# 3,680 unused bytes per partition below the MLP's tiles, in a two-layer diffusion backbone on one core

## The chip, the cores and the metric

One core of one Trainium2 chip. The metric is the device time of one execution in microseconds (us), median of the runs; lower is better. TensorE (PE) multiplies matrices, VectorE (DVE), ScalarE (ACT) and GpSimd (POOL) work elementwise, SyncE (SP) issues DMAs. PE reads two operands from the on-chip memory SBUF: the stationary one (the weights, loaded by LDWEIGHTS, shown as engine PEld) and the moving one, whose columns stream through. SBUF has 128 partitions; a tile's *address* below is its byte offset within each partition.

## The reference

Two layers run over 256 latent tokens and 256 context tokens of width 1024. Each layer ends in a squared-ReLU MLP, for both token streams in the first layer (512 tokens) and for the latent tokens alone in the last (256):

```python
def sqrelu_mlp(h, w1, w2):
    return jnp.square(jax.nn.relu(h @ w1)) @ w2
...
        x = x + mod[2][..., None, :] * (y @ w_out[l])
        x = x + mod[5][..., None, :] * sqrelu_mlp(ada_norm(x, g_mlp[l], mod[3], mod[4]), w_ff1[l], w_ff2[l])
```

`w_ff1` is 1024 x 4096 and `w_ff2` 4096 x 1024. Before the MLP stand a combined input projection (`w_in`), differential attention, latent attention, a bidirectional HGRN2 scan and an output projection (`w_out`).

## The kernel before

Activations are held with features on partitions and tokens along the free dimension, so a linear layer has the weights as stationary operand (128 x 128) and 512 or 256 tokens as moving operand. Every float32 product is made from three float32r products: weights and activations are each split into a high part and the rest, and `mm3` issues (weights x activations) high x high (L140), high x rest (L141) and rest x high (L142):

```python
139    def mm3(ps, lh, ll, rh, rl, start, stop):
140        PE.matmul(ps, lh, rh, start=start, stop=False)
141        PE.matmul(ps, lh, rl, start=False, stop=False)
142        PE.matmul(ps, ll, rh, start=False, stop=stop)
```

`wunit` (L120) fetches 512 KB of weights by a DMA on SP's queue into one of four `raw` buffers; ACT copies it to `wh` (L135, the high part), DVE subtracts to get `wl` (L136, the rest). `wh` and `wl` have three buffers each. `lin_fm` (L144) walks over such units: in the MLP a unit has 4 k-tiles of 256 output columns, so 24 matmuls (4 k-tiles x 2 column blocks x 3) read it.

The linear layers differ in the tile that they stream: the input projection reads `hh` and `hl`, the output projection `yh` and `yl`, the MLP's first product `mhh` and `mhl` (8 x 512 floats each; class `Norm` writes them), its second `fa` and `fb` (16 buffers each, written in `ev_ff`: L1334 and L1335). The MLP runs in two groups of 2048 hidden columns (L1318), each 16 units of `w_ff1` and then 16 of `w_ff2`: 64 units, 1,536 matmuls in a layer. In layer 0 `mod_beside` (L411) runs beside it on DVE: it sums the next layer's conditioning from `w_mod` (L424, L426), one DMA and two DVE instructions per step. The order on every engine is the order in which this Python issues.

The moving operand is 512 columns wide in layer 0 (`Tq` = 512). In layer 1 `fa` and `fb` are 256 wide; `mhh` and `mhl` are read through `Norm.gained`, which begins two columns early (L309, `x0 = self.T0 - 2`) to carry the shift vectors along: 258 columns from column 254 on.

Tiles come from stacked pools. The pool `wp` (raw, `wh`, `wl`, and `hh`, `hl`, `yh`, `yl`) is allocated once, low in SBUF. The pools of a layer's attention are closed before the MLP's pool opens (L1308), which then takes their place, directly above what stays. The built program places:

| tiles | address | modulo 4096 |
|---|---|---|
| `wh`, `wl` (three each, 4096 apart) | 88,960 to 109,440 | 2944 |
| `hh`, `hl`, `yh`, `yl` (16,384 each, k-tiles 2048 apart) | 56,192 and 72,576 | 2944, 896 |
| `mhh`, `mhl` (16,384 each, k-tiles 2048 apart) | 126,240 and 142,624 | 3360, 1312 |
| `fa`, `fb` of layer 0 (2048 each) | 159,008 to 222,496 | 3360, 1312 |
| `fa`, `fb` of layer 1 (1024 each) | 159,008 to 190,752 | 3360, 288, 1312, 2336 |
| the latent attention's `cqh`, `cql` and their weights `uqh` in layer 0 | 126,752 to 167,200, and 153,888 | |

A block of weights that a matmul loads begins 512 bytes after another inside `wh`, so all eight multiples of 512 occur as distances between weights and moving operand. The remainder by 512 does not change within a pool: `wh` lies at 384 modulo 512 and so do `hh`, `hl`, `yh`, `yl`; `mhh`, `mhl`, `fa` and `fb` at 288. In the latent attention `cqh`, `cql` and `uqh` all lie at 32 modulo 64, above the MLP pool's lower end.

Of the kernel before, what the change touches and what calls it, by code (L numbers as in the profile page):

```python
# [8 lines left out]
F32 = mybir.dt.float32  # L9
# [31 lines left out]
def net(ctx: ExitStack, tc, x, c, cx, c_ctx, w_mod, b_mod, g_mix, g_mlp, w_in, w_out, da_lambda, da_subln_g,  # L41
# [410 lines left out]
    def drain(g):  # L452
        for _ in g:
            pass
# [137 lines left out]
    def layer(l):  # L592
# [17 lines left out]
        def step(g):  # L610
            try:
                next(g)
                return True
            except StopIteration:
                return False
# [391 lines left out]
        def ev_res(gofs, k0, sq):  # L1007
            def ev(i, ps):
                k = k0 + i
                for r, a, b in streams:  # L1010
                    V.scalar_tensor_tensor(out=xT[:, k, a:b], in0=ps[:, a - T0q:b - T0q],
                                           scalar=modT[l][:, r, gofs + k:gofs + k + 1], in1=xT[:, k, a:b],
                                           op0=ALU.mult, op1=ALU.add)
                if sq:
                    sq_update(k, T0q)
            return ev
# [289 lines left out]


        with tc.tile_pool(name=f"mlp{l}", bufs=1) as fp:  # L1308
            NM = Norm(l, 1, T0q, fp.tile([128, KT, 512], F32R, name="mhh"), fp.tile([128, KT, 512], F32R, name="mhl"))
            drain(final)  # L1310
            beside = None if last else mod_beside(1)

            def run(g):
                for _ in g:
                    if beside:
                        next(beside, None)

            for grp in range(2):  # L1318
                hid = {}

                def ev_ff(j0):
                    def ev(i, ps, sp=None):
                        a = fp.tile([128, Tq], F32R, tag="fa", name="fa", bufs=16)
                        b = fp.tile([128, Tq], F32R, tag="fb", name="fb", bufs=16)
                        if sp is None:
                            t = ap_.tile([128, 512], F32, tag="ntmp", name="fr", bufs=2)
                            S.activation(out=t[:, 0:Tq], in_=ps, func=AF.Relu)
                        else:
                            t, c = NM.apply(ps, sp)
                            for r, x0, x1 in streams:  # L1330
                                tt = t[:, x0 - T0q:x1 - T0q]
                                S.activation(out=tt, in_=tt, func=AF.Relu, bias=c[:, r:r + 1])
                        V.tensor_mul(out=t[:, 0:Tq], in0=t[:, 0:Tq], in1=t[:, 0:Tq])
                        S.copy(out=a[:, 0:Tq], in_=t[:, 0:Tq])  # L1334
                        V.tensor_sub(out=b[:, 0:Tq], in0=t[:, 0:Tq], in1=a[:, 0:Tq].bitcast(F32))  # L1335
                        hid[j0 + i] = (a, b)
                    return ev

                if grp == 0:
                    drain(NM.first(w_ff1[l], [(0, 512)], ev_ff(0), not last))  # L1340
                for cc in range(0 if grp else 2, 8):
                    ev = ev_ff(2 * cc)
                    if last:
                        run(lin_fm(w_ff1[l], 0, [(2048 * grp + 256 * cc, 256)], KT, NM.gained, Tq + 2,
                                   lambda i, ps: ev(i, ps, 0)))
                    else:
                        run(lin_fm(w_ff1[l], 0, [(2048 * grp + 256 * cc, 256)], KT, NM.parts, Tq, ev))
                rhs_f = lambda k: (hid[k][0][:, 0:Tq], hid[k][1][:, 0:Tq])
                for cc in range(4):
                    g = lin_fm(w_ff2[l], 2048 * grp, [(256 * cc, 256)], 16, rhs_f, Tq, ev_res(40, 2 * cc, grp == 1))  # L1350
                    if last and grp and cc == 3:
                        step(g)
                        step(g)
                        obs = [fp.tile([128, 1024], F32, name=f"ob{t}") for t in range(2)]
                        final_rows(range(6), obs)
                    run(g)
            if beside:
                drain(beside)
            if last:
                final_norm(obs)  # L1360
# [4 lines left out]
    def final_rows(ks, obs):  # L1365

        for k in ks:
            S.activation(out=xT[:, k, 256:], in_=xT[:, k, 256:], func=AF.Copy, scale=vT2[:, k:k + 1])
        for t in range(2):
            for k in ks:  # L1370
                h = t, k // 4
                if h not in turned_x:
                    turned_x[h] = psum("mm" if k // 4 else "sc")
                PE.transpose(turned_x[h][:, 128 * (k % 4):128 * (k % 4) + 128], xT[:, k, 256 + 128 * t:384 + 128 * t], ident)
        if ks[0] == 0:
            for t in range(2):
                (V.tensor_copy, S.copy)[t](out=obs[t][:, 0:512], in_=turned_x[t, 0])

    def final_norm(obs):
        ss = stats([acc_state["a"], acc_state["b"]], 2)  # L1380
        r = rstd_small(ss, 2, DM)
        final_rows(range(6, 8), obs)
        for t, q in enumerate((nc.sync, nc.scalar)):
            V.tensor_scalar(out=obs[t][:, 0:512], in0=obs[t][:, 0:512], scalar1=r[:, t:t + 1], scalar2=None, op0=ALU.mult)
            S.activation(out=obs[t][:, 512:1024], in_=turned_x[t, 1], func=AF.Copy, scale=r[:, t:t + 1])
            for hf in range(2):
                q.dma_start(out=out[0, 128 * t:128 * t + 128, 512 * hf:512 * hf + 512], in_=obs[t][:, 512 * hf:512 * hf + 512])

    fillers += [mod_group(0, 1), mod_group(0, 2)]
    layer(0)  # L1390
    fill_all()
    layer(1)


# [49 lines left out]
```

## Time and profile before

| | us |
|---|---|
| median of 3 runs | 1242.29 (1239.74 to 1244.79) |
| the profiled execution, whole | 1242.65 |
| its span, from the first to the last instruction | 1240.9 |
| PE busy in the span | 1201.3 (97%) |
| layer 0's MLP, from its first matmul to its last | 404.46 to 782.02 |
| layer 1's MLP, likewise | 1046.44 to 1230.84 |

Times in the trace count from the span's start. A row of the timeline gives start and duration; matmuls overlap in a pipeline and their ends are modelled, so the pace of a stream is read from starts: last start minus first start, divided by the number of steps. This is called the **step** below.

### The profile page before, as it was taken

What the parts mean: (1) busy time and instruction counts of PE and PEld (TensorE: products, weight loads), DVE (VectorE), ACT (ScalarE), POOL (GpSimd) and SP (SyncE); (2) the same over time, 40 slices, a digit from 0 to 9 for tenths busy, and PEclk for the clock granted to TensorE, in tenths of its full rate; (3) what the DMA queues carried; (4) which work ended last, traced back from release to release, by engine and by line L of the source; (5) the groups of instructions that cost most, each with busy time, mean ns of one, the idle gap of its engine ahead of it and who ended that gap; (6) DMA issues with size and microseconds to landing.
All of it is one profiled execution on the core that took longest, in us unless ns stands there. A gap on an engine that the chain in (4) does not pass through costs nothing.

```text
span 1240.9 us, 21471 instructions
## 1 busy us (share of the span) xinstructions
PE 1201.3 (97%) x8318; PEld 963.9 (78%) x8318; DVE 888.5 (72%) x1786; ACT 584.4 (47%) x1114; POOL 111.4 (9%) x156
## 2 busy tenths in 40 slices
PE   6999999999999999999999999999998998999997
PEld 4677888755568777878787877788986668999997
DVE  4675587767776997765778673796788877865864
ACT  3534344576653654211233322464347874653653
POOL 2200000221200100000000000140003421000000
PEclk9999999999999999999999999999999998999999
DMA  9631213456543346555555554233324413555662
GB/s 324 187 86 49 76 53 105 119 158 198 189 153 107 98 139 198 188 154 159 178 155 162 164 169 134 68 103 99 94 58 121 126 32 119 175 184 187 187 187 69
DMA packets 138199, 170.93 MB, mean 138 GB/s; under 512 B 10883, under 2 KB 116033, under 8 KB 138097
## 3 DMA queue, kind: packets, MB, share of 16 engines
q1 hardware_dynamic: 134816, 164.08, 43.8%
q0 software_dynamic: 2704, 4.94, 1.6%
q8 instruction: 66, 1.08, 0.4%
q10 hardware_dynamic: 576, 0.53, 0.1%
q14 instruction: 37, 0.30, 0.1%
HBM read 160.21 MB, written 1.05 MB: 130 GB/s over the span
## 4 chain that ended last, share of the span: by engine, by line
PE 85%; DVE 7%; DMA 3%; ACT 3%; POOL 1%; issue 1%; ACTq 0%; POOLq 0%; SPq 0%
PE mm L142 21%; PE mm L140 21%; PE mm L141 21%; PE sc L1239 3%; PE sc L1225 2%; PE mm L392 2%; PE tp L907 2%; PE mm L219 2%; PE mm L218 2%; PE mm L220 2%; DMA mraw<-in_w_mod_dram 2%; PE sc L797 1%; DMA raw<-in_w_in_dram 1%; PE mm L930 1%; DVE wl L136 1%; PE sc L691 1%
## 5 line engine op out<-in xcount | busy, mean ns | idle before, releaser
L135 ACT CAST wh<-raw 128x1024 fp32r<-128x1024 f32 (+2 forms) x204 | 211.0, 1035 | 315.4 <-PE mm L141 244.9
L136 DVE TENSOR_TENSOR wl<-raw,wh 128x1024 fp32r<-128x1024 f32 (+2 forms) x201 | 242.9, 1209 | 127.5 <-ACT wh L135 124.7
L140 PE MATMUL mm<-mhh,wh 128*128 128x512 f32 (+1 forms) x512 | 174.0, 340 | 0.8 <-DVE fz L336 0.8
L140 PE MATMUL mm<-fa,wh 128*128 128x512 f32 (+1 forms) x512 | 173.7, 340 | 0.0
L142 PE MATMUL mm<-mhh,wl 128*128 128x512 f32 (+1 forms) x512 | 173.0, 339 | 0.4 <-DVE wl L136 0.4
L141 PE MATMUL mm<-mhl,wh 128*128 128x512 f32 (+1 forms) x512 | 173.3, 338 | 0.0
L141 PE MATMUL mm<-fb,wh 128*128 128x512 f32 (+1 forms) x512 | 173.3, 339 | 0.0
L142 PE MATMUL mm<-fa,wl 128*128 128x512 f32 (+1 forms) x512 | 173.2, 339 | 0.0
L426 DVE SCALAR_TENSOR_TENSOR room<-raw,scm,room 128x1024 f32<-128x1024 f32 x84 | 106.4, 1287 | 39.8 <-DMA raw<-in_w_mod_dram 39.8
L140 PE MATMUL mm<-hh,wh 128*128 128x512 f32 (+1 forms) x336 | 126.7, 382 | 4.6 <-ACT hh L351 3.3
L141 PE MATMUL mm<-hl,wh 128*128 128x512 f32 (+1 forms) x336 | 126.8, 378 | 2.3 <-DVE hl L352 2.3
L142 PE MATMUL mm<-hh,wl 128*128 128x512 f32 (+1 forms) x336 | 126.8, 378 | 1.1 <-DVE wl L136 1.1
L140 PEld LDWEIGHTS mm<-mhh,wh 128*128 128x128 f32 x512 | 96.2, 188 | 15.5 <-ACT wh L135 2.5
L140 PEld LDWEIGHTS mm<-fa,wh 128*128 128x128 f32 x512 | 96.3, 188 | 14.2 <-ACT wh L135 2.5
L142 PEld LDWEIGHTS mm<-mhh,wl 128*128 128x128 f32 x512 | 96.3, 188 | 12.5 <-DVE wl L136 0.8
L142 PEld LDWEIGHTS mm<-fa,wl 128*128 128x128 f32 x512 | 96.4, 188 | 11.7
L141 PEld LDWEIGHTS mm<-fb,wh 128*128 128x128 f32 x512 | 96.5, 189 | 11.6
L141 PEld LDWEIGHTS mm<-mhl,wh 128*128 128x128 f32 x512 | 96.3, 188 | 11.2
L140 PEld LDWEIGHTS mm<-hh,wh 128*128 128x128 f32 x336 | 63.5, 190 | 15.6 <-ACT hh L351 4.2
L141 PEld LDWEIGHTS mm<-hl,wh 128*128 128x128 f32 x336 | 64.2, 191 | 14.0 <-DVE hl L352 4.1
L142 PEld LDWEIGHTS mm<-hh,wl 128*128 128x128 f32 x336 | 64.0, 191 | 13.2 <-DVE wl L136 2.0
L347 POOL TENSOR_TENSOR nt<-nt,bc 128x256 f32<-128x256 f32 x24 | 27.0, 1132 | 493.5 <-ACT bc L326 445.5
(333 smaller groups left out, 2189.8 us busy)
## 6 DMA issues: line engine op xcount, KB each, us to landing
raw<-in_w_ff_dram SPq DMA_DIRECT2D x128, 512.0 KB, 3.8
raw<-in_w_mod_dram SPq DMA_DIRECT2D x80, 512.0 KB, 3.7
raw<-in_w_in_dram SPq DMA_DIRECT2D x42, 512.0 KB, 3.8
mraw<-in_w_mod_dram SPq DMA_DIRECT2D x32, 256.0 KB, 6.0
raw<-in_w_out_dram SPq DMA_DIRECT2D x10, 512.0 KB, 3.7
raw<-in_w_in_dram SPq DMA_DIRECT2D x16, 256.0 KB, 5.1
raw<-in_w_in_dram SPq DMA_DIRECT2D x8, 384.0 KB, 3.3
K<-dah POOLq DMA_DIRECT2D x48, 64.0 KB, 2.3
```

What stands on the lines that cost most here:

```text
L135: S.copy(out=wh, in_=raw)
L136: (low.pop() if low else V).tensor_sub(out=wl, in0=raw, in1=wh.bitcast(F32))
L140: PE.matmul(ps, lh, rh, start=start, stop=False)
L141: PE.matmul(ps, lh, rl, start=False, stop=False)
L142: PE.matmul(ps, ll, rh, start=False, stop=stop)
L218: PE.matmul(ps, a, wh[:, k, 0:w], start=st, stop=False)
L219: PE.matmul(ps, a, wl[:, k, 0:w], start=False, stop=False)
L220: PE.matmul(ps, b, wh[:, k, 0:w], start=False, stop=sp)
L347: G.tensor_mul(out=ts, in0=ts, in1=self.bc[:, a - T0:b - T0])
L392: PE.matmul(ps[32 * j:32 * j + 32, :], scm[:, k, :], raw[:, 512 * q:512 * q + 512], start=(k == 0), stop=(k == KT - 1))
L426: V.scalar_tensor_tensor(out=acc[r], in0=raw, scalar=scm[:, k, r:r + 1], in1=acc[r], op0=ALU.mult, op1=ALU.add)
L1239: PE.matmul(op[64 * r:64 * r + 64, 0:128], v[:, j, 64 * c:64 * c + 64], PT[:, js], start=(j == 0), stop=(j == nk - 1), tile_position=(0, 6 ...
```

## The change

Inside the MLP's pool, ahead of all its tiles, 920 floats per partition are allocated and never used:

```diff
         with tc.tile_pool(name=f"mlp{l}", bufs=1) as fp:
+            fp.tile([128, 920], F32, name="gap")
             NM = Norm(l, 1, T0q, fp.tile([128, KT, 512], F32R, name="mhh"), fp.tile([128, KT, 512], F32R, name="mhl"))
             drain(final)
```

All tiles of that pool, in both layers, move up by 3,680 bytes. In the changed program `mhh` and `mhl` lie at 129,920 and 146,304 (2944 and, every other k-tile, 896 modulo 4096), `fa` and `fb` of layer 0 from 162,688 on (2944 and 896), those of layer 1 from 162,688 on (2944, 3968, 896 and 1920). All of these are 384 modulo 512, as `wh` and `wl` are. Layer 1's slices of `mhh` and `mhl` begin 254 columns in, at 376 modulo 512 (before: 280).

No instruction is added, removed or moved on any engine, and on PE, DVE, ACT and SP every instruction waits for the same semaphores at the same counts as before. On POOL, at the start of layer 1, the first L654 no longer waits for twelve DMA semaphores beside PE and ACT, and the first K-tile DMAs of L888 wait for DMA semaphores that this instruction had waited for.

## Rows read from the trace of the kernel before

**Rows 1.** The page: span, busy time by engine, the chain that ended last by engine.
```profile
span 1240.9 us, 21471 instructions
PE 1201.3 (97%) x8318; PEld 963.9 (78%) x8318; DVE 888.5 (72%) x1786; ACT 584.4 (47%) x1114; POOL 111.4 (9%) x156
...
PE 85%; DVE 7%; DMA 3%; ACT 3%; POOL 1%; issue 1%; ACTq 0%; POOLq 0%; SPq 0%
```

**Rows 2.** Windows by stage: stretch, length, busy time (instructions) of PE, PEld, DVE, ACT, POOL; PEclk, DMA.
```profile
404.46:443.06 38.60, 37.04 (x166) 27.90 (x165) 36.49 (x75) 25.93 (x52) 6.74 (x8) 1.00 0.23 69
443.06:782.02 338.96, 338.96 (x1476) 267.39 (x1475) 237.35 (x274) 104.24 (x138) 0.00 (x0) 1.00 0.55 166
...
1046.44:1230.84 184.40, 184.25 (x1554) 183.76 (x1554) 126.08 (x236) 96.56 (x150) 0.00 (x0) 1.00 0.55 169
```

**Rows 3.** The chain of waits, 443 to 782: its shares by line.
```profile
by line: PE mm L142 32.7%; PE mm L140 32.7%; PE mm L141 32.3%; PE sc L433 1.8%; PE tp L440 0.6%
```

**Rows 4.** Waits of PE, then of ACT, 443 to 782: total us, times, longest.
```profile
PE mm L142 <- DVE wl L136: 0.4, 1, 0.4
...
ACT wh L135 <- PE mm L141: 133.9, 42, 5.8
```

**Rows 5.** Timeline of PE, layer 0: streams of yh, yl, then mhh, mhl (start, duration).
```profile
372.03 0.40 PE L141 MATMUL mm<-yl,wh 128*128 128x512 f32 x1
...
404.46 0.40 PE L140 MATMUL mm<-mhh,wh 128*128 128x512 f32 x1
...
443.06 0.40 PE L140 MATMUL mm<-mhh,wh 128*128 128x512 f32 x1
...
485.70 0.40 PE L142 MATMUL mm<-mhh,wl 128*128 128x512 f32 x1
```

**Rows 6.** Timeline of PE: the last long fa, fb stream, then layer 1's hh, hl.
```profile
724.84 0.40 PE L141 MATMUL mm<-fb,wh 128*128 128x512 f32 x1
...
774.97 0.40 PE L142 MATMUL mm<-fa,wl 128*128 128x512 f32 x1
...
789.98 0.39 PE L141 MATMUL mm<-hl,wh 128*128 128x512 f32 x1
...
795.20 0.39 PE L156 MATMUL sc<-wh,shs 128*32 128x512 f32 x1
```

**Rows 7.** Timeline of PE: six matmuls of layer 0's latent attention and their successor.
```profile
241.97 0.39 PE L140 MATMUL mm<-cqh,uqh 128*96 128x512 f32 x1
...
243.33 0.34 PE L1206 MATMUL mm<-ukh,ckh 128*128 128x384 f32 x1
```

**Rows 8.** Windows with the tile mm alone: stretch, length, PE busy (matmuls), PEclk, DMA.
```profile
443.06:782.02 338.96, 332.44 (x1408) 1.00 0.55 166
```

**Rows 9.** Windows in layer 0's MLP, columns as in rows 2.
```profile
440.00:460.00 20.00, 19.60 (x84) 15.30 (x83) 19.55 (x24) 10.45 (x18) 0.00 (x0) 1.00 0.58 168
```

**Rows 10.** Timeline of DVE and PE: one wl, and the first matmul that reads it.
```profile
449.13 1.22 DVE L136 TENSOR_TENSOR wl<-raw,wh 128x1024 fp32r<-128x1024 f32 x1
...
452.67 0.39 PE L142 MATMUL mm<-mhh,wl 128*128 128x512 f32 x1
```

**Rows 11.** Timeline of PE, layer 1: streams of yh, yl, of mhh, mhl, of fa, fb.
```profile
1037.35 0.28 PE L142 MATMUL mm<-yh,wl 128*128 128x256 f32 x1
...
1046.22 0.28 PE L142 MATMUL mm<-yh,wl 128*128 128x256 f32 x1
...
1138.84 0.29 PE L140 MATMUL mm<-mhh,wh 128*128 128x258 f32 x1
...
1184.08 0.28 PE L140 MATMUL mm<-fa,wh 128*128 128x256 f32 x1
...
1223.83 0.29 PE L142 MATMUL mm<-fa,wl 128*128 128x256 f32 x1
```

**Rows 12.** Timeline of POOL at the start of layer 1.
```profile
810.65 4.10 POOL L347 TENSOR_TENSOR nt<-nt,bc 128x256 f32<-128x256 f32 x1
814.74 3.60 POOL L654 TENSOR_SCALAR KE<-KE,oml 128x512 f32<-128x512 f32 x2
```

## The prediction, made before the changed kernel was timed

> **What bounds the kernel now.** Read the page first: PE is busy 97% of a span of 1240.9 us and holds 85% of the chain that ended last [rows 1]. So the time is PE's, except where it waits. Then the windows by stage [rows 2]: layer 0's MLP is 38.60 us in which PE is not always busy (37.04) and DVE nearly is (36.49), then 338.96 us in which PE is busy throughout; layer 1's MLP is 184.40 us with PE busy 184.25. The two MLPs are 561.96 us, 45% of the span, and they are the only stages whose tiles the change moves. In the long stretch the chain of waits is 98% matmuls of the three lines of mm3 [rows 3]; PE waits once, 0.4 us at its start [rows 4], while ACT waits 133.9 us in all for PE to give weight buffers back [rows 4]. Nothing feeds PE too late there: what a matmul costs is what the stage costs.
>
> So the question is the step from one matmul to the next, and it differs between streams of the same shape. yh, yl, 512 columns: from 372.03 to 404.46 there are 143 steps, 32.43 / 143 = 226.8 ns. At 404.46 the output projection gives way to the MLP with no pause, and mhh, mhl take 42.64 us for 182 steps from 443.06 to 485.70, 234.3 ns [rows 5]. fa, fb: 50.13 us for 214 steps, 234.3 ns. Back at hh, hl in layer 1: 5.22 us for 23 steps, 227.0 ns [rows 6]. Shape, weights and lines are the same in all four, and the granted clock in the MLP's windows is 1.00, the level of 2.4 GHz [rows 2]. What differs is the moving tile. Those with the step of 227 lie at the weights' remainder modulo 512 (384), those with 234 do not (288). The modulus 4096 in the change's description matters less than it says: the weights that a unit loads begin at every multiple of 512, so already now a stream meets all eight distances, and the step does not follow them.
>
> Is it the place in SBUF rather than the offset, since the MLP's tiles lie above 126,240? The latent attention's cqh, cql lie there too, at their weights' remainder modulo 64 (32): six matmuls take 243.33 - 241.97 = 1.36 us, 226.7 ns each [rows 7]. That is short, but it is the fast step from high tiles. With 64 as the modulus this row and the others agree: remainders equal, 227; 32 apart, 234.
>
> **The change part by part.** No instruction comes or goes; only addresses and two POOL waits differ. The sum is made against the profiled execution, 1242.65 us; the median of the runs shown, 1242.29, is 0.4 lower, which is less than their spread (5.05).
>
> *Layer 0, the long stretch.* From 443.06 to 782.02 the window counts 1408 matmuls [rows 8], one of them begun before: 1407. All of mhh, mhl, fa, fb then lie as hh, hl, yh, yl do. The rows have no MLP matmul at that offset, so bounds first. Below: 512 columns at the granted 2.4 GHz stream in 213.3 ns, 21.0 less than now: -29.5 us. Above: nothing gained, 0, or, if the shift went the wrong way by the same 7.5 ns that it should gain, +10.6. The nearest row is the stream with the same shape and offsets, 226.8: 1407 x (234.3 - 226.8) = -10.6 us. The Trainium skill (TensorE: Matmul & The Clock Gate, "Step-by-step: what each phase is for") speaks against this: TensorE has two independent SBUF read ports, and loading the next weights takes no read bandwidth from the running matmul, so their relative place should not matter and this term would be 0. The trace does not agree with that being all: 226.8 and 234.3 ns stand in one stream of PE at 404.46.
>
> Can the others follow? The stage would shrink by 3.1%. Where DVE is fullest, from 440 to 460, it is busy 19.55 of 20 us [rows 9]. The tightest weights after 443 are a wl that ends at 449.13 + 1.22 = 450.35 and is first read at 452.67, 2.32 us later [rows 10]; by then PE has gained 41 steps x 7.5 = 0.3 us. DMA's share is 0.55 [rows 2] and would be 0.57. So nothing comes late, and the 10.6 us stand. If DVE did hold PE up over those 20 us, 85 steps' gain, 0.6 us, would go.
>
> *Layer 0, the first 38.6 us.* 129 matmuls; PE loses 1.56 us there and DVE has 36.49 of 38.60 [rows 2], writing the norm's outputs that the matmuls wait for. A faster matmul only waits longer: I take 0, with -1.0 (129 x 7.5) as the other end.
>
> *Layer 1, fa and fb, 256 columns.* 768 matmuls. Here the relation is the other way round: yh, yl at the weights' remainder take 8.87 / 74 = 119.9 ns, fa, fb off it 39.75 / 335 = 118.7 [rows 11]. The nearest row for the moved tiles is again yh, yl: 768 x 1.2 = +0.9 us.
>
> *Layer 1, mhh and mhl, 258 columns.* 768 matmuls, now 45.24 / 384 = 117.8 ns [rows 11]. No row has this width at another offset, and the slice begins 254 columns in, so the change takes it from 280 to 376 modulo 512, 8 bytes short of the weights' 384 rather than on it. Bounds: 258 / 2.4 = 107.5 ns below, -7.9 us; above, that plus the 21.0 ns that the slow 512-column step has over its columns, 128.5 ns, +8.2 us. Two rows are near: its own, 117.8, if an uneven start is what counts, and yh, yl's 119.9 plus two columns, 120.7, if nearness to the weights' offset does. Neither is nearer, so I take the middle, 119.25: +1.1 us.
>
> *POOL's waits.* The first L654 began at 814.74, when the L347 ahead of it ended [rows 12]: its long list of DMA waits cost nothing and its going gives nothing. The K DMAs that inherit two of them are far behind transfers of layer 0. 0.
>
> Elementwise work on the moved tiles and the gap itself: 0, no instruction reads or writes the gap. Sum: 1242.65 - 10.6 + 0.9 + 1.1 = 1234.05; I say **1234.0 us**, 0.7% below the median. After the MLP of layer 0 everything simply begins 10.6 us earlier: the next stage's first matmul follows the last one of the MLP with no wait.
>
> **The rivals.** About 0.5%, 6.2 us, is what a measurement of this kernel can tell from no change; faster means below 1236.1 and slower above 1248.5.
>
> *No change, 1242.6.* The step of 234.3 belongs to something else about the MLP's stream (its pool's place, its own access order), and the offset does not count. The Trainium skill's port rule, named above, ends here too. For it: no row shows an MLP matmul at the other offset, and in layer 1 the same difference of offsets costs nothing. Against it: the step changes with the tile on one engine at 404.46, and returns at 789.98. The layer-1 terms may still apply, so it gives 1240.5 to 1245. Chance 0.14.
>
> *Only half answers, 1238.8.* The offset could matter for one kind of tile alone, for instance through the tiles' different spacing. 768 of the 1,536 are fa, fb: 768 x 7.5 = 5.8; 1242.65 - 5.8 + 0.9 + 1.1 = 1238.8. For it: fa and fb are single buffers of 2048, mhh and mhl blocks of 16,384. Against: both have 234.3 now. Chance 0.06.
>
> *Slower, 1251.8.* In layer 1 a smaller offset to the weights costs the 258-column stream what a bad offset costs the wide one: 128.5 ns a step, +8.2, with +0.9 from fa and fb, and layer 0 gains nothing. For it: at 256 columns the equal offset is already the slower one. Against: only by 1.2 ns, and the wide rows gain. It decides from a step of about 124.7 ns on (6.2 - 0.9 = 5.3 us over 768 matmuls, 6.9 ns each) while layer 0 stands still; with layer 0's gain even 128.5 ns would leave 1241.2. Chance 0.05.
>
> **How the numbers follow.** The forecast, all of layer 0's long stretch at 226.8, has 0.75. Its own range: the 258-column step between its two rows (-1.1 to +1.1), the first stretch (-1.0), DVE's 0.6, and some 2 us for the measurement (the runs shown lie 2.5 either side of their median), not all at once: 1230.5 to 1237.5. To hold 8 in 10 it must reach over the half case and the lower edge of no change: 1230 to 1241. Faster: most of the forecast's range lies below 1236.1, 0.68, and a little of the half case, 0.01: 0.69. Slower: 0.05. The same: the rest, 0.26.
>
> **What would show it.** In the changed profile: steps of 226 to 227 ns in long streams of mhh, mhl and of fa, fb in layer 0; that MLP ending some 10.6 us earlier, with no new wait of PE for wl; fa, fb of layer 1 at 119.9 and mhh, mhl between 117.8 and 120.7; the first 38.6 us and all stages outside the MLPs as long as before. The forecast is wrong if the steps stay at 234.3, if only one pair of tiles falls to 227, if DVE or DMA appear in PE's waits after 443, or if the 258-column step leaves 117.8 to 120.7.

## The result and the profile after

| | before | after |
|---|---|---|
| median of the runs | 1243.49 us (1239.74 to 1245.49, 6 runs) | 1235.14 us (1233.96 to 1237.44, 6 runs) |
| the profiled execution, whole | 1242.65 us | 1233.96 us |
| its span | 1240.9 us | 1232.1 us |

The ratio is 0.9936, with a 95% interval of 0.9919 to 0.9952: faster, by 0.5 to 0.8%. The forecast was 1234.0 us.

The page of the changed kernel, against [rows 1]: span, busy time by engine, and the chain that ended last by engine.

```profile
span 1232.1 us, 21466 instructions
...
PE 1192.5 (97%) x8318; PEld 964.9 (78%) x8318; DVE 886.3 (72%) x1786; ACT 581.8 (47%) x1114; POOL 111.4 (9%) x156
...
PE 85%; DVE 8%; ACT 3%; POOL 1%; issue 1%; DMA 1%; SPq 0%; POOLq 0%; ACTq 0%; DVEq 0%
```

PE executes the same 8,318 matmuls in 8.8 us less; no other engine's work changed by more than 3 us. The windows by stage say where. The columns are those of [rows 2]: stretch, length, busy time (instructions) of PE, PEld, DVE, ACT, POOL, then PEclk, DMA share, GB/s. The third row is the stage between the two MLPs.

```profile
403.40:441.62 38.22, 36.45 (x166) 27.84 (x165) 36.55 (x75) 25.95 (x52) 6.71 (x8) 1.00 0.23 69
441.62:771.54 329.92, 329.12 (x1477) 266.32 (x1475) 235.17 (x274) 101.71 (x138) 0.00 (x0) 1.00 0.56 171
771.54:1035.88 264.34, 250.47 (x1990) 205.62 (x1988) 213.34 (x510) 150.28 (x314) 57.68 (x69) 0.99 0.32 88
1035.88:1222.11 186.23, 186.13 (x1554) 185.68 (x1554) 126.11 (x236) 96.48 (x150) 0.00 (x0) 1.00 0.54 168
```

The long stretch of layer 0 went from 338.96 to 329.92 us (-9.0), the first stretch from 38.60 to 38.22 (-0.4), layer 1's MLP from 184.40 to 186.23 (+1.8). The stage between them was 1046.44 - 782.02 = 264.42 and is 264.34. The rest of the difference is 1.06 us ahead of the first MLP (404.46 against 403.40), where the two kernels are the same. It is noise: in the profiles of the other kernels below that have the same code ahead of it, this point lies between 402.02 and 406.09.

The cause shows in the step. These are windows of the changed kernel with the tile mm alone (stretch, length, PE busy with its matmuls): a stream of mhh, mhl and one of fa, fb in layer 0, then one of each in layer 1, from the start of a stream's first matmul to the start of the one after its last.

```profile
441.62:482.89 41.27, 41.27 (x183) 34.16 (x182) 0.00 (x0) 4.76 (x8) 1.00 0.69 204
...
716.09:764.64 48.55, 48.55 (x215) 40.16 (x214) 3.48 (x8) 0.00 (x0) 1.00 0.55 164
1129.13:1174.86 45.73, 45.73 (x387) 45.73 (x385) 6.85 (x31) 0.00 (x0) 1.00 0.60 185
1174.86:1215.17 40.31, 40.31 (x338) 40.27 (x336) 3.68 (x10) 0.00 (x0) 1.00 0.48 144
```

A stretch counts matmuls that are still in the pipeline when it begins, so its number of steps is a little below the count: 182 and 214 in layer 0; in layer 1, 16 units of 24 = 384 and 14 units = 336. Thus 41.27 / 182 = 226.8 ns and 48.55 / 214 = 226.9 ns, where [rows 5, 6] had 234.3; 45.73 / 384 = 119.1 ns, where [rows 11] had 117.8; 40.31 / 336 = 120.0 ns, where [rows 11] had 118.7.

One thing is new. The waits of PE from 441.6 to 772 (total us, times, longest), against [rows 4], which had the second row only:

```profile
PE tp L440 <- DVE modsb L436: 0.8, 1, 0.8
PE mm L142 <- DVE wl L136: 0.4, 1, 0.4
```

Its place, in the timeline of PE: the transposes of `mod_beside` begin 1.15 us after the matmul ahead of them (0.24 us in all six rounds of the kernel before), and the unit after them can only follow.

```profile
714.22 0.39 PE L142 MATMUL mm<-fa,wl 128*128 128x512 f32 x1
715.37 0.66 PE L440 MATMUL tp<-ident,modsb 128*128 128x128 f32 x4 [0.76 <-DVE modsb L436]
```

Against those 0.24 us, 0.9 us is lost here and another 0.2 us at 657.87, where the same transposes begin 0.42 us after the matmul ahead: 1.1 us together.

### The profile page after: what moved, and what is told of

It is laid out like the page before. It is cut to its first block, busy times and chain, and to the rows that moved or that the text cites. A ratio compares the mean times of both kernels' runs of the same rounds, so it can differ in the third digit from the quotient of the medians.

```text
span 1232.1 us, 21466 instructions
## 1 busy us (share of the span) xinstructions
PE 1192.5 (97%) x8318; PEld 964.9 (78%) x8318; DVE 886.3 (72%) x1786; ACT 581.8 (47%) x1114; POOL 111.4 (9%) x156
## 4 chain that ended last, share of the span: by engine, by line
PE 85%; DVE 8%; ACT 3%; POOL 1%; issue 1%; DMA 1%; SPq 0%; POOLq 0%; ACTq 0%; DVEq 0%
PE mm L140 21%; PE mm L142 21%; PE mm L141 20%; PE sc L1239 3%; PE sc L1225 2%; PE mm L392 2%; PE tp L907 2%; PE mm L218 2%; PE mm L219 2%; PE mm L220 2%; DVE wl L136 1%; PE sc L797 1%; PE mm L930 1%; PE sc L768 1%; PE sc L691 1%
## 5 line engine op out<-in xcount | busy, mean ns | idle before, releaser
L426 DVE SCALAR_TENSOR_TENSOR room<-raw,scm,room 128x1024 f32<-128x1024 f32 x84 | 106.4, 1287 | 57.1 <-DMA raw<-in_w_mod_dram 57.1
```

Source lines behind the costliest of these rows:

```text
L426: V.scalar_tensor_tensor(out=acc[r], in0=raw, scalar=scm[:, k, r:r + 1], in1=acc[r], op0=ALU.mult, op1=ALU.add)
```

## The experiments

Three questions were open: whether it is really the offset between moving tile and weights, and by which modulus; whether layer 1's loss comes from the same thing; and whether the new wait belongs to the change. Below, *offset* is the moving tile's address minus that of the weights. The kernels are the kernel before with the edit shown, unless stated. All stream rows have the columns of the windows with the tile mm above; for a stream cut at its last step, the steps are 182, 214, 305, 289, 384 and 335.

### A gap of 32 bytes

```diff
         with tc.tile_pool(name=f"mlp{l}", bufs=1) as fp:
+            fp.tile([128, 8], F32, name="gap")
```

> The gap is 32 bytes instead of 3,680: the MLP's tiles then lie at the weights' remainder modulo 64, but 64 bytes off modulo 512. Theory A (the remainder modulo 64 of moving tile against weights counts): layer 0's long streams of mhh, mhl and fa, fb step at 226.7 ns, layer 1's fa, fb at 119.9 and mhh, mhl at about 119.1, and the time is that of the change, 1235 us. Theory B (512 or 4096 counts): 234.3 ns in layer 0, 118.7 and 117.8 in layer 1, 1243 us.

Measured: 1238.45 us (ratio 0.9972, 0.9956 to 0.9989). The windows show streams of mhh, mhl and of fa, fb in layer 0, and the same in layer 1:

```profile
442.00:484.47 42.47, 42.47 (x183) 34.22 (x182) 0.00 (x0) 4.79 (x8) 1.00 0.66 200
722.67:772.60 49.93, 49.93 (x215) 40.23 (x214) 3.50 (x8) 0.00 (x0) 1.00 0.47 146
1135.66:1181.75 46.09, 46.09 (x387) 46.09 (x386) 6.97 (x32) 0.00 (x0) 1.00 0.60 184
1181.75:1219.73 37.98, 37.98 (x337) 37.98 (x336) 3.62 (x10) 0.00 (x0) 1.00 0.51 153
```

42.47 / 182 = 233.4 and 49.93 / 214 = 233.3 ns: the remainder modulo 64 is equal and the stream is slow. Theory A, the prediction's, falls. Theory B's numbers fail too: 256 columns take 37.98 / 335 = 113.4 ns, faster than any row of before, and 258 columns 46.09 / 384 = 120.0. An offset of -64 bytes is bad for 512 columns and the best yet for 256.

### A gap of 64 bytes, and everything 32 bytes up

The first has `fp.tile([128, 16], ...)` as gap. The second leaves the MLP's pool alone and puts 32 bytes below all tiles:

```diff
+    const.tile([128, 8], F32, name="gap")
     ident = const.tile([128, 128], F32, name="ident")
```

> The gap is 64 bytes: the MLP's tiles stay 32 bytes off the weights modulo 64. Theory A: every step as in the kernel before (234.3 ns in layer 0; 118.7 and 117.8 in layer 1), about 1243 us. Theory C (that the pool's tiles move at all, or begin elsewhere, is what helped, not the offset): 226.7 ns, about 1235 us.

> The kernel before with 32 unused bytes below everything, so that weights and all streamed tiles move up by 32 bytes together; every distance stays. Theory A (distance to the weights counts): all steps as before, hh, yh 226.7 ns, mhh, fa 234.3 ns in layer 0, about 1243 us. Theory D (the moving tile's own address modulo 64 counts, 0 good and 32 bad): the other way round, mhh, fa 226.7 ns and hh, yh 234.3 ns, about 1239 us.

One run each: 1239.42 and 1243.02 us. With the 64-byte gap, mhh, mhl of layer 0, then of layer 1:

```profile
440.55:483.02 42.47, 42.47 (x184) 34.19 (x182) 0.00 (x0) 4.77 (x8) 1.00 0.65 200
1134.91:1180.99 46.08, 46.08 (x386) 46.08 (x385) 6.89 (x31) 0.00 (x0) 1.00 0.59 184
```

233.4 ns, so moving the pool alone gives next to nothing (theory C falls); but theory A's 234.3 and 117.8 are missed as well, the 258 columns taking 120.0. The total of 1239.4 is one run, and its stages ahead of the MLP were 2.4 us shorter than in the profile of before, with the same code; the steps decide, not the total.

With everything 32 bytes up, yh, yl and then mhh, mhl:

```profile
372.82:405.24 32.42, 32.42 (x144) 26.84 (x143) 4.97 (x12) 0.00 (x0) 1.00 0.37 114
443.83:486.47 42.64, 42.64 (x183) 34.28 (x182) 0.00 (x0) 4.76 (x8) 1.00 0.66 199
```

32.42 / 143 = 226.7 and 42.64 / 182 = 234.3, as in [rows 5] (226.8 and 234.3). Here mhh lies at the very address that it had with the 32-byte gap (233.4 ns there); what differs is that the weights, and all else below the MLP's pool, moved along. So it is the offset to the weights that counts, not the moving tile's address: theory D falls.

### The gap in layer 0 alone, and modsb on ACT

```diff
+            if not last:
+                fp.tile([128, 920], F32, name="gap")
```

> The change's gap in layer 0 alone; layer 1's tiles keep their old places. Theory A: layer 0 as in the change (226.7 ns, MLP 368 us), layer 1's MLP back to 184.8 us from 186.6 (fa, fb 118.7, mhh, mhl 117.8 ns): 1.8 us less than the change, 1233.3 us. Rival: layer 1's 1.8 us do not come from the offset (a later start of its work, say), then its MLP stays at 186.6 us and the time at 1235.

The second experiment adds, to this one, in `mod_beside`:

```diff
-            V.tensor_copy(out=sb, in_=ps)
+            S.copy(out=sb, in_=ps)
```

> The gap in layer 0 alone, and mod_beside's copy out of PSUM (L436) on ACT instead of DVE. In the changed kernel PE waited twice for that copy, about 1.1 us together, which it had not done before. Theory: the copy stood behind DVE's other work, and with a faster PE it comes late; on ACT, which is idle most of that stretch, it does not: no wait of PE's transposes for modsb, layer 0's MLP at most 367.0 us (it was 366.9 with the gap in layer 0 alone and 368.1 in the change), 1230.5 us. Rival: the waits vary from run to run whichever engine copies, or ACT's copy delays wh: no gain or up to 1 us slower than with the gap in layer 0 alone.

The gap in layer 0 alone: 1230.78 us, ratio 0.9903 (0.9886 to 0.9920). Its stages:

```profile
404.58:442.81 38.23, 36.47 (x167) 27.84 (x165) 36.46 (x75) 25.94 (x52) 6.72 (x8) 1.00 0.22 69
442.81:771.51 328.70, 328.70 (x1476) 266.54 (x1475) 236.38 (x274) 103.74 (x138) 0.00 (x0) 1.00 0.55 171
1035.91:1219.92 184.01, 183.94 (x1555) 183.43 (x1554) 126.17 (x236) 96.56 (x150) 0.00 (x0) 1.00 0.55 170
```

Layer 1's MLP is back at 184.0 us, so its loss was the offset's. Layer 0 took 366.9 us and, in this run, PE did not wait for modsb at all, although layer 0's program is the changed kernel's: 328.70 is 10.3 us below the 338.96 of [rows 2].

With the copy on ACT: 1231.35 us, ratio 0.9908 (0.9892 to 0.9924), no different. The view of the tile modsb has, for the copies and for the transposes (duration min/median/max, first and last start):

```profile
L440 PE MATMUL tp<-ident,modsb x24: 270/272/273, 489.0 to 769.9; 128*128 128x128 f32 x24
...
L436 ACT COPY modsb<-sc x6: 588/588/591, 483.5 to 764.1; 128x512 f32<-128x512 f32 x6
```

Worked out from the timeline, the copy's end leads the first transposes by 4.86 us in each of the six rounds. On DVE this lead is, round by round, 2.6, 3.8, 4.0, 3.9, 3.9, 4.0 us in the kernel before; 2.0, 3.5, 3.7, 3.0, 3.2, 3.8 with the gap in layer 0 alone; and 1.7, 2.2, 1.8, 0.1, 0.1, 3.8 in the changed kernel. With the gaps of 32 and 64 bytes and with everything up, whose layer 0 is slow, it stands at 3.9 from the second round on. So DVE's lead shrinks where PE is faster. The changed kernel's timeline of DVE shows how it ran out (start, duration; in brackets the idle time before and what ended it):

```profile
704.07 1.29 DVE L426 SCALAR_TENSOR_TENSOR room<-raw,scm,room 128x1024 f32<-128x1024 f32 x1 [3.95 <-DMA raw<-in_w_mod_dram]
...
714.63 0.69 DVE L436 COPY modsb<-sc 128x512 f32<-128x512 f32 x1
```

DVE stood 3.95 us until a `w_mod` DMA landed, and what was queued behind, the copy at its end, came that much later. Over the long stretch L426 of DVE waited 57.1 us for such DMAs in the changed kernel (longest 3.9), against 39.8 (2.7) in the kernel before and 44.2 (2.4) with the gap in layer 0 alone, where PE did not wait. So the wait is not certain, but its room is gone; with the copy on ACT it did not come. The time cannot show it, since the kernel compared with had no such wait in its profile.

### Many offsets

Two kernels spread the offsets within one kernel, k-tile by k-tile: `mhh`, `mhl` with a k-tile stride of 2048 + 64 (then + 8) bytes, and `fa`, `fb` with a gap after every second pair of buffers in layer 0, after every pair in layer 1.

```diff
+            mh = [fp.tile([128, KT, 528], F32R, name="mhh")[:, :, 0:512]]
...
+            for j in range(16):
+                for t in "ab":
+                    fp.tile([128, Tq], F32R, tag=f"f{t}{j}", name="f" + t, bufs=1)
+                if last:
+                    fp.tile([128, 8], F32, name=f"gap4_{j}")
+                elif j % 2:
+                    fp.tile([128, 16], F32, name=f"gap4_{j}")
```

> One look at many offsets: the MLP's tiles are laid out so that the streamed k-tiles lie 0, 64, ... 448 bytes from the weights' remainder modulo 512 (mhh, mhl by k; fa, fb of layer 0 by pairs of k), and 0, 32, ... 480 bytes for fa, fb of layer 1; the pool begins 96 bytes up, so the remainder modulo 4096 is not the weights'. Theory A2 (the remainder modulo 512 counts, symmetric): 512 columns 226.7 ns at 0, 233.3 at 64 and 448, about 234 between; 256 columns 120.0 at 0, 113.9 at 64 and 448, about 118 at 32 and 480. Theory B2 (the whole remainder modulo 4096 counts): no stream at 226.7. Theory C2 (the sign counts): 64 differs from 448 by more than 1 ns.

> The same in steps of 8 bytes around the equal offset: mhh, mhl at 0 to 56 bytes in layer 0 (258 columns: -8 to 48), fa, fb of layer 0 at -64 to -8 by pairs, fa, fb of layer 1 at -128 to -8. Theory A3 (a unit of 64 bytes or so counts: any offset within it behaves like 0): 512 columns 226.7 ns up to some offset, then a jump to 233.3. Theory B3 (the cost grows with the offset): the step rises by steps of 8 bytes from 226.7 to 233.3. For 256 columns: 120.0 near 0 and 113.9 at -64, with the place of the fall between.

1240.41 and 1241.29 us, one run each, and no answer of the kind that was meant: the offset changes every three or six matmuls, and no stream settles. In the second kernel the gaps of `fa`, `fb` were also rounded up to 32 bytes. In the first one's timeline, six matmuls of fa, fb at the offset 256 (723.35 to the start of the next six):

```profile
723.35 0.40 PE L140 MATMUL mm<-fa,wh 128*128 128x512 f32 x1
...
724.74 0.40 PE L140 MATMUL mm<-fa,wh 128*128 128x512 f32 x1
```

1.39 / 6 = 231.7 ns, with single steps between 224 and 236. Yet the first told one thing: averaged by the place among the six, the steps at offset 0 and at 256 agree (230.1, 233.1, 231.0, 234.4, 227.2, 229.2 against 230.3, 233.1, 230.9, 234.6, 227.2, 229.1), and so do 64 and 320, 128 and 384, 192 and 448, within 0.9 ns. Offset 64 against 448 differs (231.0 and 233.7 on average). That points to a modulus of 256 and to a sign, and asks for constant offsets per stream.

Three kernels give each stream one offset, by gaps ahead of `mhh` and ahead of `fa` and, in layer 1, slices of wider tiles; layer 1's two groups read `fa`, `fb` at different places. The pattern of the edit, here with the gaps of the first:

```diff
+            X, FW = (2, 64) if last else (0, 0)
+            FX = (8, 0) if last else (0, 0)
+            mh = []
+            for t, g in (("mhh", 72 if last else 88), ("mhl", 120 if last else 0), ("", 80 if last else 96)):
+                if g:
+                    fp.tile([128, g], F32, name="gap_" + t)
+                if t:
+                    mh.append(fp.tile([128, KT * 512 + X], F32R, name=t)[:, X:].rearrange("p (k f) -> p k f", k=KT))
...
+                        f0 = FX[grp]
+                        a = fp.tile([128, Tq + FW], F32R, tag="fa", name="fa", bufs=16)[:, f0:f0 + Tq]
```

> Constant offsets per stream, for streams long enough to settle (offset: moving tile minus weights). Layer 0: mhh, mhl at 256 bytes, fa, fb at 128. Layer 1: mhh, mhl (258 columns) at 192, fa, fb at 64 in the first group and 32 in the second. Theory E (the remainder modulo 256 counts): layer 0's mhh, mhl step at 226.7 ns although they are 256 bytes off modulo 512. Theory F (modulo 512): 233 to 235 ns. For the other streams no offset of these has been seen: Theory E only says that 512 columns at 128 are slower than 226.7; the 256 columns may lie anywhere from 113.5 to 120.5.

> As before, other offsets. Layer 0: mhh, mhl at 64, fa, fb at 32 bytes. Layer 1: mhh, mhl (258) at 0, fa, fb at 128 and 96. Theory E: layer 0 slower than 226.7 ns in both, 230 to 235. If the cost is symmetric about the equal offset (64 like 192, 32 like 224), both give 233.3. 258 columns at 0: 119 to 120 if the equal offset is the slow one for short streams, as with 256 columns (120.0).

> As before, other offsets. Layer 0: mhh, mhl at 96, fa, fb at 0 with mhh, mhl off it. Layer 1: mhh, mhl (258) at 128, fa, fb at 192 and 200. Theory E: fa, fb of layer 0 at 226.7 ns, mhh, mhl 233 to 235; fa, fb of layer 1 at 192 step at 113.6 ns, as at 448 before (the same modulo 256); under theory F (modulo 512) 192 is a new place. 200: 113.6 if the 64-byte unit counts, else more.

The first (1237.08 us): layer 0's mhh, mhl at 256; fa, fb at 128; layer 1's mhh, mhl at 192; fa, fb at 64 in the first group and, in the last row, at 32.

```profile
441.90:483.18 41.28, 41.28 (x183) 34.17 (x182) 0.00 (x0) 4.76 (x8) 1.00 0.64 204
...
718.35:768.08 49.73, 49.73 (x216) 40.32 (x214) 3.50 (x8) 0.00 (x0) 1.00 0.50 148
1132.48:1178.88 46.40, 46.40 (x387) 46.40 (x386) 6.95 (x31) 0.00 (x0) 1.00 0.59 182
...
1178.88:1218.33 39.45, 39.45 (x337) 39.45 (x336) 3.58 (x9) 0.00 (x0) 1.00 0.47 147
```

The second (1241.37 us): layer 0's mhh, mhl at 64; fa, fb at 32; layer 1's mhh, mhl at 0, in the first group and in the second; fa, fb at 128 in the first group and, in the last row, at 96.

```profile
441.93:483.59 41.66, 41.66 (x183) 34.18 (x182) 0.00 (x0) 4.78 (x8) 1.00 0.65 202
719.86:769.78 49.92, 49.92 (x215) 40.10 (x214) 3.50 (x8) 0.00 (x0) 1.00 0.49 147
1053.56:1090.41 36.85, 36.85 (x307) 36.85 (x306) 6.25 (x26) 0.00 (x0) 1.00 0.61 182
1136.25:1182.32 46.07, 46.07 (x386) 46.07 (x385) 6.89 (x31) 0.00 (x0) 1.00 0.59 183
...
1182.32:1222.52 40.20, 40.20 (x338) 40.20 (x336) 3.63 (x10) 0.00 (x0) 1.00 0.46 145
```

The third (1239.19 us): layer 0's mhh, mhl at 96; fa, fb at 0; layer 1's mhh, mhl at 128; fa, fb at 192 and at 200.

```profile
444.66:487.13 42.47, 42.47 (x184) 34.16 (x182) 0.00 (x0) 4.78 (x8) 1.00 0.62 198
722.01:770.56 48.55, 48.55 (x216) 40.16 (x214) 3.50 (x8) 0.00 (x0) 1.00 0.49 151
1133.18:1180.12 46.94, 46.94 (x387) 46.94 (x385) 7.36 (x32) 0.00 (x0) 1.00 0.56 181
1100.41:1133.18 32.77, 32.77 (x290) 32.77 (x290) 3.19 (x7) 0.00 (x0) 1.00 0.61 192
1180.12:1220.32 40.20, 40.20 (x338) 40.20 (x336) 3.57 (x9) 0.00 (x0) 1.00 0.44 145
```

41.28 / 182 = 226.8 at 256 bytes: theory F (512) falls, theory E (256) holds. It holds again at 192, where 256 columns take 32.77 / 289 = 113.4 ns, as they did at 448; in that stream the tiles lie by turns at 192 and at 448 modulo 512, and the pace is even. All steps in long streams, in ns, of all kernels but the two of the spread offsets, the next section's included:

| offset modulo 256 | 512 columns | 256 columns | 258 columns |
|---|---|---|---|
| 0 | **226.8** | 120.0 | 120.8, 120.0 |
| 32 | 233.3 | 117.8 | |
| 64 | 228.9 | 117.8 | |
| 96 | 233.3 | 120.0 | |
| 128 | 233.3, 232.4 | 118.7 | 122.2 |
| 152 | | | **117.8**, 121.1 |
| 160 (fa, fb before) | 234.3 | 118.7, 117.3 | |
| 184 | | | 120.0 |
| 192 | 233.3 | **113.4**, 117.8 | 120.8 |
| 200 | | 120.0 | |
| 216 | | | 120.0 |
| 224 | 233.3 | 118.3 | |
| 248 (mhh in layer 1 after) | | | 119.1, 120.0 |

The cost is not symmetric about 0: 64 and 192 give 228.9 and 233.3 ns at 512 columns, 117.8 and 113.4 at 256 (32 and 224 do agree at 512 columns). And 8 bytes, 192 to 200, cost 256 columns 6.6 ns in these streams; 120.0 is neither pace that was seen at 192. The guesses of a 64-byte unit and of a symmetric cost fall.

### The best offsets, and the change again

The first is the gap in layer 0 alone, and in layer 1 32 bytes between `mhl` and `fa`:

```diff
+            if not last:
+                fp.tile([128, 920], F32, name="gap")
             NM = Norm(l, 1, T0q, fp.tile([128, KT, 512], F32R, name="mhh"), fp.tile([128, KT, 512], F32R, name="mhl"))
+            if last:
+                fp.tile([128, 8], F32, name="gap")
```

> The version that the offsets point to: layer 0 with the change's gap (offset 0), layer 1 without it, but 32 bytes between mhl and fa, so that mhh, mhl stay at 152 (117.8 ns) and fa, fb lie at 192 modulo 256 (113.5 ns). Theory E: layer 1's MLP 184.4 - 768 x (118.3 - 113.5 = 4.8 ns) = 180.7 us, the time 3.7 us below that of the gap in layer 0 alone: 1227 us. Rival: in layer 1 something else, weights or their conversion, becomes the limit once fa, fb are faster: PE waits for wh or wl there, and less than half of the 3.7 us is left.

> The changed kernel once more, unaltered, beside the version above. If PE's two waits for modsb (1.1 us) belong to the change, they are there again and layer 0's MLP takes 368.1 us; if they vary from run to run, they may be gone and it takes 366.9, as it did with the gap in layer 0 alone. Time 1235 us in the first case, 1234 in the second.

The first: 1229.49 us, ratio 0.9895 (0.9878 to 0.9912). That beats both kernels, but it cannot be told from the gap in layer 0 alone (0.9903). In its profiled run, the slowest of its four (1233.2 us; the others took 1229.3 to 1229.6; it was late by 1.5 us already at its first MLP, 406.06 against 404.58 with the gap in layer 0 alone), layer 1's streams were, in order, mhh, fa in the first group and mhh, fa in the second:

```profile
1048.67:1084.61 35.94, 35.94 (x306) 35.94 (x306) 6.30 (x26) 0.00 (x0) 1.00 0.59 186
1096.10:1130.13 34.03, 34.03 (x290) 34.03 (x290) 3.28 (x7) 0.00 (x0) 1.00 0.61 186
1130.13:1176.63 46.50, 46.50 (x386) 46.50 (x385) 6.97 (x31) 0.00 (x0) 1.00 0.59 182
1176.63:1214.62 37.99, 37.99 (x338) 37.99 (x336) 3.58 (x9) 0.00 (x0) 1.00 0.47 153
```

117.8, 117.8, 121.1 and 113.4 ns. Layer 1's MLP took 183.4 us there, where 180.7 were expected and 184.0 stood with the gap in layer 0 alone. The offsets of the two groups are the same. So the rival with late weights is wrong (the rows show PE busy throughout), and theory E is not enough either: one offset can run at two paces.

The change again: 1235.59 us, ratio 0.9938 (0.9924 to 0.9953). Its wait for modsb, its long stretch of layer 0 by the windows by stage, and, with the tile mm alone, its first long stream of mhh, mhl in layer 1:

```profile
PE tp L440 <- DVE modsb L436: 0.6, 1, 0.6
```

```profile
440.84:770.67 329.83, 329.15 (x1476) 266.31 (x1475) 235.26 (x274) 101.82 (x138) 0.00 (x0) 1.00 0.56 171
```

```profile
1045.71:1082.31 36.60, 36.60 (x307) 36.60 (x306) 6.30 (x26) 0.00 (x0) 1.00 0.59 182
```

With 329.83 it repeats the change's 329.92, so of the two cases expected the first holds. The third row is 36.60 / 305 = 120.0 ns, where the same stream of the same program took 119.0 in the profile of the change. The wait was there in three of the four profiles that have layer 0's program as the change has it and DVE copying (0.8, 0.6, 0.8 us, and none).

## Why the prediction was right, and where not

*What bounds the kernel.* Right. PE's step was the only thing that changed, and the time followed it.

*Layer 0, the long stretch: -10.6.* The step went to 226.8, as forecast from yh, yl. Measured -9.0, or -10.3 where the new wait did not come (the gap in layer 0 alone). Two things were left out. The wait of PE's transposes for modsb took 1.1 us; the prediction had looked at DVE only around 440 to 460 and at weights, and listed a wait for DVE after 443 as a sign against it. There it was wrong: what came late was the conditioning's copy behind `w_mod`'s DMAs, in a lead that had been ample. The other 0.3 us lie in the restarts: in each of `mod_beside`'s six rounds, 22 steps after its first interruption average 228.0 ns instead of 226.7, and in five some 24 steps after its second 227.6 to 228.6: (6 x 22 + 5 x 24) x 1.3 ns = 0.3 us. In the kernel before they do not differ (234.3).

*The reason.* Half right. The offset between moving tile and weights does count, as the experiment with everything 32 bytes up shows. But "with 64 as the modulus this row and the others agree" was the step that failed: a gap that keeps the remainder modulo 64 equal gave 233.3 ns. The modulus is 256, as far as the steps tell (0 and 256 agree, and 192 and 448; 64 and 128 do not serve). The row of cqh [rows 7] could not tell: `cqh` and `uqh` are 153,888 - 126,752 = 27,136 = 106 x 256 bytes apart, so they agree by both moduli. Theory and forecast gave the same number for this change only because it makes the offset 0 by every modulus up to 512.

*The first 38.6 us: 0.* Measured -0.4, inside its two ends. *POOL's waits: 0.* The stage between the MLPs is 264.34 against 264.42. *Elementwise work: 0.* The prediction's reason speaks of the gap alone, not of what writes the moved tiles; but in layer 0 ACT's copies to fa take 621 ns before and after, DVE's subtractions to fb 687 and 689.

*Layer 1: +0.9 and +1.1.* Measured +1.8 for the MLP: fa, fb 120.0 - 118.7 = 1.3 ns, mhh, mhl 119.1 - 117.8 = 1.3 ns, each 768 times 1.0 us. The middle taken for 258 columns, 119.25, was close, by luck: the table shows that neither nearness to offset 0 nor an uneven start sets it, and the change's second profile has 120.0 in one of its two groups.

*The rivals.* "No change" and the slower case fell with the first row of steps, "only half answers" too, since both kinds of tile run at 226.8. The Trainium skill (TensorE: Matmul & The Clock Gate, "Step-by-step: what each phase is for") gives the two read ports as independent; the runs disagree at least with the conclusion, drawn from it in the prediction, that addresses do not matter: 226.8 and 234.3 ns for the same 512 columns, by the offset alone.

*The sum.* 1234.05 against 1233.96 in the profiled execution and 1235.14 in the median. The hit is partly luck: the noise of -1.06 ahead of the MLP cancels the wait of 1.1 us.

## What to carry to other kernels

Where PE is the bound, compare its step between streams of the same shape: a difference of a few ns on thousands of matmuls, with no wait in sight, can come from where the moving tile lies against the weights, and then a gap changes it. Nothing is special about 3,680 bytes: 352 did the same for mhh, mhl in the first kernel with one offset per stream. The good offset depends on the width (512 columns wanted 0 modulo 256, 256 columns 192), so one shift for all layers is not the best: leaving layer 1 out saved 2.2 us of its MLP. And when the bound engine speeds up by 3%, look at the leads of everything that feeds it, the side work included, not only of what feeds its main loop.

## What the runs showed of the hardware that was not expected

- The step depends on the offset of the moving tile to the weights modulo 256, by up to 7.5 ns at 512 columns (226.8 to 234.3) and 6.6 ns at 256 (113.4 to 120.0), at a granted clock of 1.00 in all these streams. The same remainder modulo 64 or 128 is not enough. At 512 columns and offset 0 all seven profiles that have such a stream in the MLP settle at 226.7.
- It is a property of a settled stream. Where the offset changes every six matmuls, even those at the good offset take 230.9 ns on average.
- It does not come from ACT and DVE writing other buffers of `wh` and `wl` meanwhile: in the last long fa, fb stream of the kernel before, the steps within such a write average 234.3 ns, and so do those with none.
- The same offset can run at two paces in different stretches of one run: 256 columns at 192 took 113.4 and 117.8 ns, at 160 117.3 and 118.7; 258 columns at 152 took 117.8 and 121.1. The pace changes where a stream starts or is disturbed: in the kernel with the 32-byte gap, 256 columns ran at 117.7 ns from 1091.42 to 1101.20 and, after two long steps (196 and 223 ns), at 113.3, with the same tiles at the same offset. Within undisturbed stretches of the MLP, after their first 24 steps, the averages over 24 steps stay within 0.7 ns. What selects the pace is open; it was not tried. It may be part of why executions of one kernel differ by several us, which was not shown either.
- Why the offset matters is open too: the runs show that it does, not by what path in the chip.
